# Two filler rates, an earlier feed-forward norm, a group norm over whole tiles and another order of the second half's products in an RWKV-7/mLSTM trunk

## The chip, the cores and the metric

The kernel runs on one core of a Trainium2 chip. Its engines work from queues of their own, each in program order: TensorE (PE, with its weight loads shown as PEld), VectorE (DVE), ScalarE (ACT), GpSimd (POOL) and SyncE (SP), which issues nearly all DMAs. The metric is the device time of one execution, in microseconds; lower is better. TensorE's clock is granted at one of two levels, 1.2 or 2.4 GHz; the profile shows the granted clock of a stretch as a share of the full one.

## What is computed

A two-layer trunk over 1024 tokens of width 1024. Layer 0 mixes tokens with RWKV-7, layer 1 with mLSTM, and each is followed by a SwiGLU feed-forward. The change touches layer 0's mixer and the start of its feed-forward:

```
xs = x[None] + xx[None] * mix[:, None, None, :]          # six mixes of each token with the one before
r, wl, k, v, al, gl = (xs[i] @ w_in[:, off:off + n] ...)  # receptance, decay, keys, values, rate, gates
decay = exp(-exp(-softplus(-(w0 + tanh(wl) @ w2)) - 0.5)); a = sigmoid(a0 + al @ a2); g = sigmoid(gl) @ g2
state = state * w_t + sa * b_t + v_t * k_t;  y = state @ r_t      # one step for each token
mu = mean(y, -1); var = mean(square(y - mu), -1)                  # over the 64 channels of a head
y = ((y - mu) * rsqrt(var + GN_EPS)) * gn_w + gn_b                # group norm
x = x + g1 * (((y + bonus) * g) @ w_out)
h = _rms(x) * (1.0 + sc2) + sh2;  x = x + g2 * swiglu(h)
```

## The kernel before

All data is float32, channels on the 128 partitions and tokens in two halves of 512 on the free axis. A large product is done in three matmuls, high part by high part, high by low and low by high: `split` makes the high part on ACT and the low part on DVE, for weights (128x1024) and operands (128x512) alike.

**The steps.** `chunks` runs the recurrence in 19 steps i = 0 to 18. Each of 16 blocks (8 head pairs of the first half of the tokens, then the 8 of the second) goes through `rw_prep` in step i, `rw_inverse` in step i+1, `rw_solve` in step i+2, and `rw_chain` and `rw_finish` in step i+3. `rw_chain` is serial: eight times it multiplies the state (PE, `c<-st,AR`), adds (DVE, tile `VU`), multiplies again (PE, `c<-VU,SR` and `c<-VU,KT`), and updates the state (DVE, tile `st`), while ACT copies the result to `Ys`. `rw_finish` takes the group norm of `Ys`, transposes it on PE, multiplies in the gates and stores it (`yd`). "Step 13" below means the stretch between the first `c<-st,AR` of the chain of i = 13 and that of i = 14.

**The filler.** Between these parts `run` draws dense products from `fillers`: the first half's values and gates, the second half's six products, the output projection of the first half, its feed-forward norm, and the first five column blocks of the feed-forward (`first`). Each `yield` reports units of PE work, some 24 matmuls of 512 columns for five of them, and `run(limit)` draws until `QUOTA` x (step + position) units are reached. `until` draws further wherever a step needs a product that isn't there. All fillers together are 317 units. `mixed` makes the operands of one product: for each of eight tiles one ACT scaling, one DVE multiply-add and a split, into the 18 buffers of the pool `a`, which hold one product's operands at a time. The products write PSUM tile `dn`.

**The order.** The instructions of an engine run in the order that the scheduler built, by data dependencies and by the place in the program. `ahead(part)` moves what it encloses forward by the number in `AHEAD`. When the steps are over, the pools are closed and opened anew (`FROOM`), and the output projection of the second half begins (`second`, `project`, with operands in `ga`).

Of the kernel before, what the change touches and what calls it, by code (L numbers as in the profile page):

```python
# [11 lines left out]
AF = mybir.ActivationFunctionType  # L12
ALU = mybir.AluOpType
ADD, SUB, MUL, MAX, MIN, POW = ALU.add, ALU.subtract, ALU.mult, ALU.max, ALU.min, ALU.pow
# [3 lines left out]
P = 128  # L18
# [9 lines left out]
DECAY = float(np.exp(-0.5))  # L28
CAP = 15.0
GROUPS = [(0, 5), (5, 5), (10, 4), (14, 4), (18, 4)]  # L30
QUOTA = 16
XW = 1
PT = "pt",
PA = "tmp",
# [4 lines left out]
POS = .25, .5, .75  # L39
# [1 line left out]
FEW = 3  # L41
LI = 3, 7, 7, 10
GT = "tmp", "tmp", "a", "ld"
AHEAD = dict(chain=50, mask=400, w=50, finish=50, pair=100, g=150, norm=500)


RES = {"x": (8, 520)}
# [82 lines left out]
class K:  # L130
# [98 lines left out]
    def ahead(self, part):  # L229
        n = AHEAD.get(part, 0)  # L230
        return self.tc.high_priority(n) if n else nullcontext()
# [425 lines left out]

    def rw_inverse(self, S):

        nc = self.nc
        SA, d0 = S["SA"], S["d0"]
        d1 = self.d1[self.nd1 % len(self.d1)]
# [68 lines left out]

    def rw_solve(self, S):

        nc = self.nc
        AR, SA = S["AR"], S["SA"]
        v = self.rload("v", S["j"], S["hf"])
        VU = self.t("VU", [P, 8, P])
# [34 lines left out]
        for e in range(2):  # L774
            nc.vector.tensor_copy(AR[:, e::2, self.rows(e)[1]], ps[e])
        S["VU"] = VU

# [22 lines left out]
    def rw_finish(self, S):  # L800

        nc = self.nc
        j, hf, Ys = S["j"], S["hf"], S["Ys"]
        y3 = Ys.rearrange("p u (h d) -> p (u h) d", h=2)
        m, v, jk = (self.t(n, [P, 64 if n == "gj" else 8]) for n in ("gm", "gv", "gj"))
        nc.vector.tensor_reduce(m, y3, mybir.AxisListType.X, ADD)
        nc.vector.tensor_scalar(m, m, -1.0 / 64, None, MUL)
        for q in range(8):
            nc.scalar.activation(jk, y3[:, q, :], AF.Square, bias=m[:, q:q + 1], accum_out=v[:, q:q + 1])
        nc.vector.tensor_scalar(v, v, 1.0 / 64, GN_EPS, MUL, ADD)  # L810
        nc.gpsimd.tensor_tensor(v, v, self.mhalf, POW)
        nc.vector.tensor_tensor(m, m, v, MUL)
        for q in range(8):
            nc.scalar.activation(y3[:, q, :], y3[:, q, :], AF.Identity, bias=m[:, q:q + 1], scale=v[:, q:q + 1])
        ps = self.bank("tr")
        for u in range(4):
            nc.tensor.transpose(ps[:, u * P:u * P + P], Ys[:, u, :], self.k_("ident"))
        bv = self.t("pt")
        nc.sync.dma_start(bv, self.bvd[j, hf])
        v = self.rload("v", j, hf)  # L820
        nc.vector.tensor_tensor(bv, bv, v, MUL)
        g = self.rload("g", j, hf)
        nc.vector.scalar_tensor_tensor(bv, ps, self.col("gn_w", j), bv, MUL, ADD)
        nc.vector.scalar_tensor_tensor(bv, bv, self.col("gn_b", j), g, ADD, MUL)
        nc.sync.dma_start(self.yd[hf][j], bv)
# [595 lines left out]
    def fillers(self, x0):  # L1421

        yield from self.rkv(0, "v")
        yield from self.gate(0)
        self.second_half()
        yield from self.lora(1, "s")
        yield from self.lora(1, "a")
        yield from self.rkv(1, "k")
        yield from self.rkv(1, "r")
        yield from self.rkv(1, "v")  # L1430
        yield from self.gate(1)
        for kt in range(KT):
            t = self.t("x")
            self.nc.sync.dma_start(t, self.A["xT"][kt, :, 0:HT])
            x0.append(t)
        while self.finished < 8:
            yield 0
        yield from self.project(self.yd[0], "wro", 0, x0, self.a0, PA)
        self.store(0, x0)
        self.norm_blocks(x0, 0, self.rstd(x0))  # L1440
        hp = []
        for x in x0:
            hi, lo = self.a0()
            self.split(hi, lo, x)
            hp.append((hi, lo))
        for n in range(EARLY[0][0], EARLY[0][1]):
            self.first(0, n, hp, ("mt", "tmp"))
            yield 11

    def chunks(self, x0):  # L1450
        fill = self.fillers(x0)
        self.pe = 0

        def step():
            w = next(fill, None)
            if w is None:
                return False
            self.pe += w
            return True

        def until(arr, j, hf):
            while self.done.get((arr, hf), 0) <= j:
                assert step()

        def run(limit):
            while self.pe < limit:
                n = self.pe
                if not step():
                    break
                if self.finished < 8 and self.pe == n and self.done.get(("g", 1)) == 8:  # L1470
                    break

        S = [None] * 16
        for i in range(19):
            if i >= 3:
                with self.ahead("chain"):
                    self.rw_chain(S[i - 3])
            run(QUOTA * (i + POS[0]))
            if 2 <= i < 18:
                until("v", (i - 2) % 8, (i - 2) // 8)  # L1480
                self.rw_solve(S[i - 2])
            run(QUOTA * (i + POS[1]))
            if 1 <= i < 17:
                self.rw_inverse(S[i - 1])
            run(QUOTA * (i + POS[2]))
            if i < 16:
                until("r", i % 8, i // 8)
                S[i] = self.rw_prep(i % 8, i // 8)
            run(QUOTA * (i + 1))
            if i >= 3:  # L1490
                until("g", (i - 3) % 8, (i - 3) // 8)
                with self.ahead("finish"):
                    self.rw_finish(S[i - 3])
                self.finished = i - 2
        while step():
            pass
# [188 lines left out]
```

## Time and profile before

| | us |
|---|---|
| median of 3 runs (lowest, highest) | 2932.73 (2917.15, 2933.27) |
| the profiled execution | 2919.56 |
| its span, first to last instruction | 2917.8 |
| PE busy | 2702.9 |
| DVE busy | 2036.1 |
| ACT busy | 1401.1 |

The span is what the engines took from the first to the last instruction; 1.8 us of the execution lie around it. An engine is busy while an instruction of its own executes. PE's busy time is no measure of speed alone: at the lower clock the same matmul takes twice as long and is busy all the while. The chains of steps 3 to 18 begin at 267.88, 318.58, 369.88, 433.77, 479.39, 516.42, 569.02, 610.01, 653.78, 715.49, 754.09, 793.62, 846.36, 882.95, 928.49 and 976.67 us.

### The profile page before, as it was taken

To read this page: it belongs to the slowest core of one execution; us is meant where nothing else is said; L and a number is where in the kernel's file an instruction comes from. 1 tells how busy PE (TensorE), PEld (TensorE's weight loads), DVE (VectorE), ACT (ScalarE), POOL (GpSimd) and SP (SyncE) were. 2 spreads that over 40 slices of the span, in tenths; PEclk is the share of its full clock that TensorE was granted. 3 is DMA by queue.
4 is the path that set the end of the run, shared out by engine and by line. 5 is a ranking of instruction groups with operands and counts; after the bars stand their busy time and mean duration, and the time that the engine had idled before them with its cause. 6 is when DMAs were issued, how large, how long until landed. Compare 5 with 4: busy or idle time off the path is not lost.

```text
span 2917.8 us, 46574 instructions
## 1 busy us (share of the span) xinstructions
PE 2702.9 (93%) x17080; PEld 2124.4 (73%) x17080; DVE 2036.1 (70%) x4029; ACT 1401.1 (48%) x2641; POOL 74.5 (3%) x98
## 2 busy tenths in 40 slices
PE   6899889999898999999999989999989999999988
PEld 5576556677676677887777767778867788887776
DVE  7877776877676468788877677665556865667645
ACT  5766786777666554322244354233435433323433
POOL 0000000000000000000000000000000000000000
PEclk9899789999798999999999989889989999999999
DMA  8775444455543455577788744345264322347734
GB/s 293 262 266 149 121 128 125 119 158 145 155 138 102 134 199 163 187 228 233 243 276 258 229 138 129 121 152 159 94 205 146 106 100 94 107 138 246 237 118 150
DMA packets 359721, 492.38 MB, mean 169 GB/s; under 512 B 125212, under 2 KB 208796, under 8 KB 359492
## 3 DMA queue, kind: packets, MB, share of 16 engines
q1 hardware_dynamic: 345668, 464.24, 50.1%
q10 hardware_dynamic: 13824, 25.17, 2.4%
q8 instruction: 134, 2.20, 0.3%
q14 instruction: 95, 0.78, 0.1%
HBM read 359.77 MB, written 129.50 MB: 168 GB/s over the span
## 4 chain that ended last, share of the span: by engine, by line
PE 61%; DVE 14%; DMA 11%; ACT 6%; issue 6%; POOL 1%; SPq 1%; DVEq 0%; POOLq 0%; ACTq 0%
PE dn L207 23%; PE c L207 20%; PE iv L207 7%; PE px L207 7%; PE sc L207 2%; DMA wraw<-wsd 2%; DMA tt<-gd 1%; DMA wraw<-in_wdn 1%; DVE wq L212 1%; DMA bgs<-in_ada 1%; DVE ga L212 1%; ACT wq L211 1%; DVE wlo L212 1%; PE tr L207 1%; ACT whi L211 1%
## 5 line engine op out<-in xcount | busy, mean ns | idle before, releaser
L207 PE MATMUL dn<-a,whi 128*128 128x512 f32 (+1 forms) x1200 | 434.4, 428 | 20.4 <-ACT a L211 8.0
L211 ACT ACTIVATE wq<-wraw 128x1024 fp32r<-128x1024 f32 x202 | 210.7, 1057 | 335.4 <-DVE wraw L889 89.6
L207 PE MATMUL c<-ga,wq 128*128 128x512 f32 x1446 | 354.2, 394 | 8.6 <-ACT ga L211 7.8
L207 PEld LDWEIGHTS c<-ga,wq 128*128 128x128 f32 x1446 | 271.5, 189 | 73.7 <-ACT ga L211 10.1
L212 DVE TENSOR_TENSOR wq<-wraw,wq 128x1024 fp32r<-128x1024 f32 x202 | 244.3, 1221 | 85.3 <-ACT wq L211 85.1
L207 PEld LDWEIGHTS dn<-a,whi 128*128 128x128 f32 (+1 forms) x1200 | 226.3, 196 | 81.8 <-ACT a L211 10.7
L207 PE MATMUL dn<-a,wlo 128*128 128x512 f32 (+1 forms) x664 | 275.1, 425 | 5.8 <-ACT wlo L443 2.9
L207 PE MATMUL c<-gb,wq 128*128 128x512 f32 x894 | 220.9, 399 | 9.4 <-DVE wq L212 6.4
L207 PEld LDWEIGHTS c<-gb,wq 128*128 128x128 f32 x894 | 169.2, 191 | 49.5 <-DVE wq L212 7.6
L207 PEld LDWEIGHTS dn<-a,wlo 128*128 128x128 f32 (+1 forms) x664 | 128.8, 197 | 37.1 <-issue 4.8
L211 ACT ACTIVATE whi<-wraw 128x1024 fp32r<-128x1024 f32 (+2 forms) x96 | 100.4, 1046 | 113.2 <-PE dn L207 81.9
L212 DVE TENSOR_TENSOR wlo<-wraw,whi 128x1024 fp32r<-128x1024 f32 (+2 forms) x96 | 116.0, 1208 | 45.7 <-ACT whi L211 39.7
L207 PE MATMUL iv<-ga,wq 128*128 128x512 f32 x552 | 136.0, 389 | 0.0
L207 PE MATMUL px<-ga,wq 128*128 128x512 f32 x528 | 128.7, 389 | 0.0
L211 ACT ACTIVATE w<-wraw 128x384 fp32r<-128x384 f32 (+1 forms) x100 | 56.7, 567 | 139.9 <-PE c L207 62.3
L207 PEld LDWEIGHTS iv<-ga,wq 128*128 128x128 f32 x552 | 103.6, 188 | 21.6
L207 PEld LDWEIGHTS px<-ga,wq 128*128 128x128 f32 x528 | 99.1, 188 | 20.7
L207 PE MATMUL dn<-gb,wq 128*128 128x512 f32 x426 | 104.1, 396 | 5.0 <-ACT gb L211 4.7
L207 PE MATMUL iv<-gb,wq 128*128 128x512 f32 x432 | 104.7, 390 | 0.0
L207 PEld LDWEIGHTS dn<-gb,wq 128*128 128x128 f32 x426 | 81.1, 191 | 23.9 <-ACT gb L211 5.3
L207 PE MATMUL c<-ga,w 128*128 128x512 f32 x372 | 93.4, 393 | 1.1 <-DVE ga L212 0.7
L1124 ACT ACTIVATE x<-x 128x512 f32<-128x512 f32 x77 | 48.3, 629 | 95.0 <-DVE x L933 44.9
(607 smaller groups left out, 5643.5 us busy)
## 6 DMA issues: line engine op xcount, KB each, us to landing
wraw<-in_wgu SPq DMA_DIRECT2D x110, 512.0 KB, 3.5
tt<-gd SPq DMA_DIRECT2D x154, 256.0 KB, 4.1
KT<-in_ada SPq DMA_DIRECT2D x40, 512.0 KB, 5.3
gd<-x SPq DMA_DIRECT2D x77, 256.0 KB, 2.0
gd<-tt SPq DMA_DIRECT2D x72, 256.0 KB, 2.1
wraw<-wsd SPq DMA_DIRECT2D x32, 512.0 KB, 4.7
bgs<-in_ada SPq DMA_DIRECT2D x96, 128.0 KB, 3.3
wraw<-in_wdn SPq DMA_DIRECT2D x24, 512.0 KB, 4.4
```

The source lines that it names most:

```text
L207: return self.nc.tensor.matmul(out, lhsT, rhs, start=start, stop=stop, **kw)
L211: self.nc.scalar.activation(hi, src, AF.Copy)
L212: self.nc.vector.tensor_tensor(lo, src, hi.bitcast(F32), SUB)
L1124: nc.scalar.activation(t, t, AF.Silu)
```

## The change

Four edits. The filler gets 19.6 units a step in the first 11 steps and 12.6 afterwards, in place of 16 throughout. The second half's products come as decay, keys, rate, receptance, gates, values, in place of decay, rate, keys, receptance, values, gates. The feed-forward norm of the first half and its split are moved forward in the schedule by 400. The group norm works on the whole 128x512 tile: DVE adds the negated mean, ACT squares once into a tile of the pool `pt`, DVE sums it and scales the tile, in place of eight ACT instructions that square and sum, and eight that scale and shift.

```
-QUOTA = 16
+
+QUOTA = 19.6, 12.6
-AHEAD = dict(chain=50, mask=400, w=50, finish=50, pair=100, g=150, norm=500)
+AHEAD = dict(chain=50, mask=400, w=50, finish=50, pair=100, g=150, norm=500, front=400)
@@ rw_finish
-        m, v, jk = (self.t(n, [P, 64 if n == "gj" else 8]) for n in ("gm", "gv", "gj"))
+        m, v = (self.t(n, [P, 8]) for n in ("gm", "gv"))
         nc.vector.tensor_reduce(m, y3, mybir.AxisListType.X, ADD)
         nc.vector.tensor_scalar(m, m, -1.0 / 64, None, MUL)
-        for q in range(8):
-            nc.scalar.activation(jk, y3[:, q, :], AF.Square, bias=m[:, q:q + 1], accum_out=v[:, q:q + 1])
+        nc.vector.tensor_tensor(y3, y3, m[:, :, None].to_broadcast([P, 8, 64]), ADD)
+        sq = self.t("pt", [P, 8, 64])
+        nc.scalar.activation(sq, y3, AF.Square)
+        nc.vector.tensor_reduce(v, sq, mybir.AxisListType.X, ADD)
         nc.vector.tensor_scalar(v, v, 1.0 / 64, GN_EPS, MUL, ADD)
         nc.gpsimd.tensor_tensor(v, v, self.mhalf, POW)
-        nc.vector.tensor_tensor(m, m, v, MUL)
-        for q in range(8):
-            nc.scalar.activation(y3[:, q, :], y3[:, q, :], AF.Identity, bias=m[:, q:q + 1], scale=v[:, q:q + 1])
+        nc.vector.tensor_tensor(y3, y3, v[:, :, None].to_broadcast([P, 8, 64]), MUL)
@@ fillers
         yield from self.lora(1, "s")
+        yield from self.rkv(1, "k")
         yield from self.lora(1, "a")
-        yield from self.rkv(1, "k")
         yield from self.rkv(1, "r")
+        yield from self.gate(1)
         yield from self.rkv(1, "v")
-        yield from self.gate(1)
...
-        self.norm_blocks(x0, 0, self.rstd(x0))
-        hp = []
-        for x in x0:
-            hi, lo = self.a0()
-            self.split(hi, lo, x)
-            hp.append((hi, lo))
+        with self.ahead("front"):
+            self.norm_blocks(x0, 0, self.rstd(x0))
+            hp = []
+            for x in x0:
+                hi, lo = self.a0()
+                self.split(hi, lo, x)
+                hp.append((hi, lo))
@@ chunks
+        def quota(x):
+            return QUOTA[0] * min(x, 11) + QUOTA[1] * max(x - 11, 0)
+
-            run(QUOTA * (i + POS[0]))
+            run(quota(i + POS[0]))
...
-            run(QUOTA * (i + 1))
+            run(quota(i + 1))
```

On PE, in the chain of step 13, the order before has the inverse of a later block (`iv`) and the products of `rw_prep` (`sc`, `c`<-`AR,KB`) between two rounds of the chain, and no filler:

```order
L207 MATMUL iv_8548<-XN_8535,SA_7990 16x16 x32
L207 MATMUL c_302_1589<-st_1582,AR_7432 128x128
L207 MATMUL iv_8585<-XB_8536,Y_1453_8547 16x16 x32
L207 MATMUL c_302_1589<-VU_8417,SR_7444 64x64 x2
L207 MATMUL c_302_1589<-VU_8417,KT_7489 64x64 x2
L207 MATMUL iv_8628<-XN_8535,SA_7990 32x32 x16
```

and the order of the changed kernel has output-projection products (`dn`) there:

```order
L208 MATMUL c_302_1589<-VU_8476,SR_7697 64x64 x2
L208 MATMUL c_302_1589<-VU_8476,KT_7742 64x64 x2
L208 MATMUL dn_8976<-a_8195,whi_8972 128x512
L208 MATMUL dn_8976<-a_8196,whi_8972 128x512
L208 MATMUL dn_8976<-a_8195,wlo_8973 128x512
L208 MATMUL dn_8976<-a_8201,whi_8972 128x512
L208 MATMUL dn_8976<-a_8202,whi_8972 128x512
L208 MATMUL c_302_1589<-st_1582,AR_7685 128x128
```

Fillers have moved into this place.

On PE, in the last chain (step 18), the order before has feed-forward products between the rounds:

```order
L207 MATMUL dn_11427<-a_10704,whi_11423 128x512
L207 MATMUL c_302_1589<-st_1582,AR_10325 128x128
L207 MATMUL dn_11427<-a_10703,wlo_11424 128x512
L207 MATMUL dn_11427<-a_10707,whi_11423 128x512
L207 MATMUL dn_11427<-a_10708,whi_11423 128x512
L207 MATMUL dn_11427<-a_10707,wlo_11424 128x512
L207 MATMUL c_302_1589<-VU_11166,SR_10337 64x64 x2
L207 MATMUL c_302_1589<-VU_11166,KT_10382 64x64 x2
```

and the changed kernel has the last inverse (`iv`), the last solve (`px`, `tr`) and then the chain with nothing between:

```order
L208 MATMUL iv_10949<-XD_10839,Y_1833_10929 32x32 x16
L208 MATMUL px_11096<-Z_11077,SA_10490 64x64
L208 MATMUL tr_11115<-SA_10490,AT_11069 64x64 x3
L208 MATMUL px_11096<-Z_11077,SA_10490 64x64 x15
L208 MATMUL tr_11115<-SA_10490,AT_11069 64x64 x5
L208 MATMUL c_302_1589<-st_1582,AR_10479 128x128
L818 MATMUL tr_11223<-kc,Ys_10994 128x128 x4
L208 MATMUL px_11116<-SA_10490,AT_11069 64x64 x8
L208 MATMUL c_302_1589<-VU_11061,SR_10491 64x64 x2
L208 MATMUL c_302_1589<-VU_11061,KT_10536 64x64 x2
L208 MATMUL c_302_1589<-st_1582,AR_10479 128x128
L208 MATMUL c_302_1589<-VU_11061,SR_10491 64x64 x2
```

All fillers now stand ahead of this chain; counted in the whole order, 130 of their matmuls stood behind its first row before, and none does now.

On DVE, in a group norm, the order before has the multiply that waits for POOL's power (L812) right behind the instruction that POOL waits for (L810), ahead of a chain's add (`VU`) and the masks (`SA`, `SR`):

```order
L810 TENSOR_SCALAR gv_8757<-gv_8757 128x8
L812 TENSOR_TENSOR gm_8756<-gm_8756,gv_8757 128x8
L787 TENSOR_TENSOR VU_8417<-c_302_1589,VU_8417 64x128
L631 TENSOR_TENSOR SA_8697<-sc_8699,kc 128x2x2x64
L631 TENSOR_TENSOR SR_8698<-sc_8699,kc 128x2x2x64
```

and the changed kernel has a sum (L812) and a scaling of the whole tile (L815) around the same wait:

```order
L812 TENSOR_REDUCE gv_7790<-pt_7794 128x8
L642 TENSOR_SCALAR br_7733<-kc,cc 128x128
L813 TENSOR_SCALAR gv_7790<-gv_7790 128x8
L788 TENSOR_TENSOR VU_7348<-c_302_1589,VU_7348 64x128
L815 TENSOR_TENSOR Ys_7247<-Ys_7247,gv_7790 128x512
L822 TENSOR_TENSOR pt_7805<-pt_7805,ld_7807 128x512
```

One instruction stands between L813 and L815 here.

## Rows read from the trace of the kernel before

**Rows 1.** The page: busy time, share of the span and instructions by engine.

```profile
PE 2702.9 (93%) x17080; PEld 2124.4 (73%) x17080; DVE 2036.1 (70%) x4029; ACT 1401.1 (48%) x2641; POOL 74.5 (3%) x98
```

**Rows 2.** Windows: stretch, length, busy per engine, granted clock, DMA share and rate.

```profile
191.58:267.88 76.30, 73.71 (x608) 56.60 (x607) 57.75 (x123) 48.45 (x81) 0.22 (x2) 1.00 0.63 183
267.88:433.77 165.89, 139.06 (x1482) 95.05 (x1481) 125.69 (x325) 129.37 (x277) 3.99 (x5) 0.85 0.44 127
433.77:569.02 135.25, 128.22 (x1498) 90.30 (x1497) 102.28 (x272) 93.66 (x227) 7.03 (x6) 0.95 0.43 123
569.02:715.49 146.47, 142.04 (x1616) 106.33 (x1613) 114.32 (x291) 102.21 (x255) 8.27 (x8) 1.00 0.53 149
715.49:846.36 130.87, 116.16 (x1399) 85.23 (x1397) 89.16 (x238) 87.67 (x221) 3.80 (x4) 0.84 0.50 150
846.36:976.67 130.31, 117.28 (x1429) 88.28 (x1426) 87.66 (x225) 80.51 (x204) 7.15 (x5) 0.90 0.41 117
976.67:1026.89 50.22, 40.31 (x236) 29.99 (x235) 23.75 (x46) 27.31 (x72) 3.27 (x2) 0.96 0.43 145
```

**Rows 3.** Windows, steps 13 and 16, all instructions.

```profile
754.09:793.62 39.53, 33.92 (x440) 25.53 (x441) 24.13 (x57) 25.66 (x71) 1.75 (x2) 0.70 0.50 161
882.95:928.49 45.54, 35.65 (x453) 27.64 (x450) 30.61 (x81) 27.33 (x70) 3.40 (x2) 0.78 0.41 118
```

**Rows 4.** Windows, fillers alone (tile dn; PE, PEld, DVE, ACT), steps 3 to 17.

```profile
267.88:976.67 708.79, 338.56 (x1083) 195.02 (x1082) 8.71 (x12) 44.11 (x73) 0.91 0.46 133
```

**Rows 5.** The chain that ended last: start, length, what; a run at full clock.

```profile
1051.39 10.88 PE c L207 x48
```

**Rows 6.** Waits, 290 to 420 us: who waited for whom, us, times, longest.

```profile
PEld dn L207 <- DVE a L212: 8.7, 13, 1.7
```

**Rows 7.** Timeline, 895 to 900 us: start, length, instruction, idle before and releaser.

```profile
895.14 0.17 DVE L812 TENSOR_TENSOR gm<-gm,gv 128x8 f32<-128x8 f32 x1 [1.44 <-POOL gv L811]
895.34 2.76 ACT L814 ACTIVATE Ys<-Ys,gm,gv 128x64 f32<-128x64 f32 x8 [1.18 <-DVE gm L812]
899.40 0.71 PE L207 MATMUL c<-st,AR 128*128 128x128 f32 x2 [4.47 <-ACT Ys L797]
```

**Rows 8.** Groups by line, 190 to 1030 us: busy us, mean ns, idle before.

```profile
L814 ACT ACTIVATE Ys<-Ys,gm,gv 128x64 f32<-128x64 f32 x128 | 45.5, 428 | 18.4 <-DVE gm L812 18.2
L809 ACT ACTIVATE gj<-Ys,gm 128x64 f32<-128x64 f32 x128 | 43.9, 343 | 11.2 <-DVE gm L807 9.0
L809 ACT ACTIVATION_READ_ACCUMULATOR gj<-Ys,gm 128x1 f32 x128 | 24.1, 188 | 0.0
L211 ACT ACTIVATE a<-mt 128x512 fp32r<-128x512 f32 x60 | 37.3, 622 | 3.0 <-DVE mt L412 2.1 <-ACT Ys L797 0.6
L806 DVE TENSOR_REDUCE gm<-Ys 128x8 f32<-128x512 f32 x16 | 10.8, 676 | 1.2 <-ACT Ys L797 1.2
L609 DVE TENSOR_TENSOR pt<-pt,pt 128x512 f32<-128x512 f32 x16 | 10.9, 683 | 0.3 <-ACT pt L608 0.3
```

**Rows 9.** Groups by line, whole span, POOL.

```profile
L811 POOL TENSOR_TENSOR gv<-gv,mhalf 128x8 f32<-128x8 f32 x16 | 30.7, 1917 | 506.5 <-DVE gv L810 436.0 <-DVE VU L787 37.9 <-DVE X L678 32.6
```

**Rows 10.** Timeline of PE, last chain to the first product behind it.

```profile
995.85 0.38 PE L207 MATMUL c<-st,AR 128*128 128x128 f32 x2
...
998.39 0.38 PE L207 MATMUL c<-st,AR 128*128 128x128 f32 x2
...
999.68 0.28 PE L207 MATMUL c<-VU,KT 128*64 128x64 f32 x2
...
1011.21 0.33 PE L817 MATMUL tr<-kc,Ys 128*128 128x128 f32 x1 [1.50 <-ACT Ys L814]
...
1025.82 0.79 PE L207 MATMUL c<-ga,wq 128*128 128x512 f32 x1 [7.05 <-ACT ga L211]
```

**Rows 11.** DMA issues, 995 to 1042 us: KB each, median us to landing.

```profile
tt<-yd SPq DMA_DIRECT2D x8, 256.0 KB, 4.4
gd<-tmp SPq DMA_DIRECT2D x2, 256.0 KB, 2.0
```

More of the change, by code (lines that the diff above doesn't have):

```diff
@@ L1481, in chunks @@
                 self.rw_solve(S[i - 2])
-            run(QUOTA * (i + POS[1]))
+            run(quota(i + POS[1]))
             if 1 <= i < 17:
                 self.rw_inverse(S[i - 1])
-            run(QUOTA * (i + POS[2]))
+            run(quota(i + POS[2]))
             if i < 16:
```

## The prediction

> **What bounds the kernel now.** The page comes first. PE is busy 93% of the span, DVE 70%, ACT 48% [rows 1], so PE is the engine to follow, and a change pays where PE idles or runs slow. The change touches the recurrence alone, so I next read windows cut at the first multiply of each third chain [rows 2]. From 267.88 to 976.67 us (steps 3 to 17, 708.8 us) the reader is to see two losses in each row: the length less PE's busy time, and the length times what the granted clock lacks to 1. Steps 3 to 5 lose 165.9 - 139.1 = 26.8 us of idle and 165.9 x 0.15 = 24.9 us of clock, 51.7 together. Likewise steps 6 to 8 lose 7.0 + 6.8 = 13.8, steps 9 to 11 4.4 + 0, steps 12 to 14 14.7 + 20.9 = 35.6, and steps 15 to 17 13.0 + 13.0 = 26.0. The sum is 131.5 us: 66 idle, 65.5 clock. The other 577 us are PE's work at full clock. The fillers are 1083 matmuls of 512 columns [rows 4]; 48 of them take 10.88 us at full clock [rows 5], 0.227 each, so 246 us. The remaining 331 us are the recurrence's own work, 22.1 a step.
>
> Where the losses lie tells their cause. Steps 13 and 16 alone lose 17.5 (5.6 + 11.9) and 19.9 us (9.9 + 10.0) [rows 3]: in the order before they hold 17 and 26 fillers, against 72 a step on average. Step 13 is starved because `until` drew gates and values early in step 11, step 16 because the norm stands between the projection and the first feed-forward product. In steps 3 to 5 fillers exist but wait for operands: four `mixed` (gates, decay, rate, keys) fall between units 40 and 76, steps 2.5 to 4.75 at 16 a step, and PE's filler weight loads wait 8.7 us in 13 pieces for DVE's split [rows 6]. Steps 9 to 11 hold two `mixed` as well, but with 300 fillers, and lose only 4.4. So losses come with thin or late filler, and the clock is at its lower level, 1.2 GHz, for part of just those stretches.
>
> **The change, part by part.** *Filler.* Counted in the built order of PE, steps 3-5, 6-8, 9-11, 12-14 and 15-17 hold 197, 215, 300, 171 and 199 fillers before, and 261, 280, 233, 231 and 192 after. That is 115 more inside, 15 more ahead of step 3, and none of the 130 behind the first row of the last chain. Work moved in: 115 x 0.227 = 26.1 us, and 15 x 0.227 = 3.4 us ahead, where PE is busy 73.7 of 76.3 us at full clock [rows 2]. Their weights' loads come earlier on SP's queue too; the DMA engines are busy 41 to 53% in steps 3 to 17 [rows 2], so I cost that at nothing. Late loads would show as ACT waiting for `wraw`.
>
> *What the losses become.* The trace has no row for this, so I bound them: at least 22 us (every group like steps 9 to 11), at most 131.5 (nothing gained). Within that I take each group by its nearest row. Steps 3 to 5 now hold two `mixed` (decay, keys) instead of most of four, and ACT is freed (below): half of 51.7, 26. Steps 6 to 8 hold two (rate, receptance) instead of one: 13.8 grows to 22. Steps 9 to 11 (gates, values) have 67 fillers fewer: 9, between their own 4.4 and 13.8. Steps 12 to 14 lose the starved step: of 35.6 the 17.5 of step 13 goes, and of the other 18.1, mostly the wait for the projection's operands, a third goes too: 12. Steps 15 to 17 have the norm early, so step 16's 19.9 goes and 6 stays, but the last inverse and solve now stand bare ahead of the last chain, which I estimate at half of step 16's loss, whose like stretch stood bare too, 10 us: 16. The sum is 85, against 131.5: -46.5 us.
>
> *Group norm.* Removed from ACT, each time: eight squares of 343 ns with accumulator reads of 188, and eight scalings of 428 [rows 8], 7.7 us, for one whole-tile square, priced as the copy of the same size, 0.62: 7.1 x 16 = 113 us less on ACT. DVE gets an add, a sum and a scaling of 512 columns, 0.68 each [rows 8], for one small multiply of 0.17 [rows 7]: 1.9 x 16 = 30 us more. ACT is never the sole bound of the five groups [rows 2], so its 113 us go off the path in the main; they pay where the chain waits behind them. Rows 7 shows that: DVE waits 1.44 us for POOL, then eight scalings hold ACT 2.76 us, the copy of `Ys` comes late and PE idles 4.47 us. Such waits are inside the 46.5. The wait of DVE for POOL stays, about 1.9 us a norm [rows 9] less what stands between; in the new order that is at most 2.1 us of work and mostly one short instruction, so DVE loses perhaps 0 to 10 us more in all. I take 0 on the path, since DVE has 26% of room in steps 3 to 17 (519 of 709 us busy, [rows 2]); its share becomes (519 + 30 + 9 for the added fillers' splits) / 688 = 81%. Queued behind it are the chain's add, the masks and the splits. Every group norm also takes one more `pt` buffer of four, whose earlier user is a factor of the same `rw_prep`, long read: nothing.
>
> *The end.* Before, from the last chain's first row to the first projection product is 976.67 to 1025.82, 49.1 us [rows 2, 10], and 130 fillers run in it (29.5 us). After, it is bare. A round takes 2.54 us with few fillers in it [rows 10]; eight of them, some at the lower clock, 21.6. From the chain's end (999.96) to the first transpose, 11.25 us before [rows 10], the new norm needs copy 0.3, sums 2 x 0.68, add and scaling 2 x 0.68, square 0.62, small ones 0.4, POOL 1.9 and some 0.9 of signals: 6.8. Transposes take 0.7. Then two DVE operations (1.5), the store of `yd` (2.0, as the like `gd`), the load (4.4) [rows 11], split and signals (2.6) make 10.5, during which PE can do the 21 products of the other seven operands, 4.8. The sum is 34.8: -14.3 us. Bounds: 30, and 44 if the projection's operands arrive no sooner than before.
>
> *Norm ahead* costs no instruction; its gain is step 16's. A new order can change how often ACT loads tables; that is hidden on an engine that is idle 30% of steps 3 to 17.
>
> The sum: +3.4 + 26.1 - 46.5 - 14.3 = -31.3 us on the profiled 2919.6 (span 2917.8 and 1.8 around it): 2888. The median shown is 13.2 above that execution. Of the four known executions two lie near 2918 and two at 2933, so I add half, 6.6: **2895 us**. Medians of this kernel tell about 1% from no change, 29 us: below 2903 counts as faster.
>
> **A rule against the rows.** Idle and lower clock go together in rows 2 and 3. The Trainium skill, "TensorE: Matmul & The Clock Gate" (Terms), puts the penalty of the lower clock at the throttled time times the missing share: that would make the 65.5 us above wholly recoverable. The trace agrees only in part: in rows 7 PE waits 4.47 us at the time the clock is low in step 16, and a wait costs the same at either clock.
>
> **Rivals.** (1) *The clock stays full.* All 65.5 us of clock loss go and a third of the idle 66: losses of 44, the end as above, so 2888 - 41 = 2847, with the offset 2854. For it: steps 9 to 11 ran at 1.00 throughout. Against: 24 fillers in step 6 and 41 in step 9 of the new order. By the page's rule just named, the clock's part of it follows. Chance 0.12. (2) *The losses only move.* Rate and receptance wait for operands in steps 6 to 8 as decay and keys did, losses stay near 120: 2888 + 35 = 2923, with the offset 2930. For it: `a` still holds one product's operands. Against: starved steps 13 and 16 are filled whatever else happens. Chance 0.27. (3) *Slower: DVE becomes the bound.* DVE waits for POOL with the chain's add behind it, and its 30 us more, with 5 more of waiting, land on the path while losses stay at 131.5: 3.4 + 26.1 - 14.3 + 35 = +50, 2970, with the offset 2976. It decides once losses pass 145 us (+28.7), DVE then being nearly always what PE waits for. Against: steps 9 to 11 ran with DVE busy 78% at a loss of 3%. Chance 0.12, for 2960 and more as for 2976. The sum above has 0.49, with losses of 65 to 105 us, so 2875 to 2915.
>
> **The numbers.** The range goes from 2857 to 2932: it holds the sum's cases (0.49), rival 2 nearly whole (0.25) and the upper half of rival 1 (0.06). Faster by over 1%: three quarters of the sum's cases and rival 1, 0.49. Within 1%: the rest of the sum's cases and rival 2, 0.39. Slower: 0.12.
>
> **What would show it.** Windows from the first chain to the last should show losses of some 85 us, steps 13 and 16 at a clock above 0.9, and steps 3 to 5 shorter than 155 us though they hold 64 more fillers. ACT should be busy some 113 us less, DVE 30 more. The last chain should run without `dn` in about 22 us, the first `ga` product following within 15. It is wrong if a group loses what it lost before, if PE's longest waits are for the new scaling (L815), or if the end takes as long as before.

## The result, and the profile after

The changed kernel takes 2961.04 us (median of 4 runs, 2956.66 to 2965.10), the kernel before 2929.65 beside it: a ratio of 1.0119 with a 95% interval of 1.0098 to 1.0141. The change makes it slower by 1.2%, 31 us, where the prediction had 2895 us.

The page of the changed kernel answers to [rows 1]:

```profile
PE 2715.5 (92%) x17080; PEld 2133.0 (72%) x17080; DVE 2064.4 (70%) x4061; ACT 1326.4 (45%) x2276; POOL 72.4 (2%) x98
```

The span is 2959.6 us, 41.8 more than before; some 10 of these are chance, because the profiled execution of before was 10 us under its median. DVE is busy 28 us more (30 were said), ACT 75 less (113 were said).

Windows cut at the same places as [rows 2]: the stretch ahead of step 3, steps 3 to 5, 6 to 8, 9 to 11, 12 to 14 and 15 to 17, and the last chain up to the first `ga` product.

```profile
191.58:273.50 81.92, 77.76 (x632) 59.68 (x630) 60.24 (x133) 50.94 (x83) 0.22 (x2) 0.98 0.61 178
273.50:443.09 169.59, 153.34 (x1543) 104.73 (x1541) 126.16 (x306) 112.35 (x214) 3.98 (x5) 0.88 0.42 125
443.09:604.03 160.94, 143.68 (x1552) 104.11 (x1551) 122.48 (x297) 102.91 (x199) 5.63 (x6) 0.90 0.46 132
604.03:743.14 139.11, 126.32 (x1503) 94.58 (x1503) 102.34 (x262) 80.82 (x167) 5.25 (x6) 0.94 0.55 161
743.14:897.63 154.49, 134.25 (x1518) 99.32 (x1517) 117.67 (x310) 77.84 (x160) 7.13 (x7) 0.88 0.41 115
897.63:1019.04 121.41, 112.10 (x1404) 82.96 (x1402) 83.93 (x212) 63.99 (x134) 7.57 (x5) 0.92 0.46 133
1019.04:1055.76 36.72, 16.49 (x104) 12.10 (x105) 19.81 (x40) 8.86 (x21) 1.95 (x1) 0.50 0.35 114
```

Counted as in the prediction (idle of PE plus what the clock lacks), the five groups lose 36.6, 33.4, 21.1, 38.8 and 19.0 us, 148.9 together, against 131.5 before and 85 predicted. Steps 3 to 17 take 745.5 us instead of 708.8. (The measure counts idle time at the lower clock one and a half times; so below I give PE's idle time and the clock apart.)

The whole of steps 3 to 17 in one window, first of the kernel before, then of the changed one, and the fillers alone (tile `dn`) of the changed one, which answer to [rows 4]:

```profile
267.88:976.67 708.79, 642.77 (x7413) 465.19 (x7413) 519.11 (x1350) 493.42 (x1180) 30.24 (x28) 0.91 0.46 133
```

```profile
273.50:1019.04 745.54, 669.68 (x7513) 485.70 (x7511) 552.58 (x1385) 437.92 (x869) 29.57 (x29) 0.90 0.46 132
...
273.50:1019.04 745.54, 364.85 (x1198) 217.62 (x1197) 12.75 (x18) 47.87 (x79) 0.90 0.46 132
```

The reader is to see where the 36.8 us come from. The fillers are busy 364.85 us instead of 338.56, 26.3 more, about what was put on the 115 that were moved in (26.1). PE's idle time did not shrink by it; it grew from 66.0 to 75.9 us, and the clock fell from 0.91 to 0.90.

Steps 9, 13, 14 and 16 of the changed kernel; 13 and 16 answer to [rows 3]:

```profile
604.03:649.27 45.24, 35.97 (x448) 26.29 (x448) 33.73 (x94) 26.13 (x56) 1.75 (x2) 0.82 0.47 136
793.19:838.18 44.99, 42.12 (x501) 30.76 (x499) 36.16 (x93) 23.16 (x48) 2.12 (x2) 0.96 0.49 142
838.18:897.63 59.45, 46.67 (x511) 35.19 (x508) 44.20 (x120) 31.59 (x64) 3.26 (x3) 0.77 0.33 92
938.15:983.28 45.13, 43.37 (x513) 31.21 (x509) 35.06 (x100) 24.09 (x50) 3.28 (x2) 1.00 0.46 131
```

Steps 13 and 16 are cured, as said (clocks of 0.96 and 1.00 for 0.70 and 0.78). But steps 9 and 14 now run at 0.82 and 0.77, with 9.3 and 12.8 us idle. In step 14 the fillers stop for 29 us, from the last product of the projection to the first one of the feed-forward, with the feed-forward norm between (eight multiplies on DVE, eight scalings on ACT):

```profile
843.95 0.39 PE L208 MATMUL dn<-a,wlo 128*128 128x512 f32 x1
...
864.86 4.87 DVE L862 TENSOR_TENSOR x<-x,sc 128x512 f32<-128x512 f32 x8 [1.71 <-PE sc L208]
866.80 5.73 ACT L863 ACTIVATE x<-x,mod,scp 128x512 f32<-128x512 f32 x8
...
873.11 0.79 PE L208 MATMUL dn<-a,whi 128*128 128x512 f32 x1 [1.61 <-ACT a L212]
```

In the kernel before, the same place lay in step 16 and took 36 us:

```profile
894.53 0.40 PE L207 MATMUL dn<-a,wlo 128*128 128x512 f32 x1
...
930.80 0.79 PE L207 MATMUL dn<-a,whi 128*128 128x512 f32 x1 [0.57 <-ACT a L211]
```

So this gap did not close: it shrank from 36 to 29 us and moved, with the fillers around it, from step 16 to step 14.

The end: windows of the 20 us from the first `ga` product on, of before and of the changed kernel.

```profile
1025.82:1045.82 20.00, 19.72 (x73) 15.69 (x74) 17.51 (x23) 13.08 (x19) 0.00 (x0) 0.83 0.86 305
```

```profile
1055.76:1075.76 20.00, 15.68 (x50) 11.82 (x51) 7.31 (x11) 5.79 (x10) 0.00 (x0) 0.81 0.56 197
```

From the last chain to the first `ga` product it takes 36.7 us instead of 49.1, 12.4 less (14.3 were said). But then PE does 50 matmuls in 20 us instead of 73; at 19.72 / 73 = 0.27 each that gives 6 us back. The timeline of PE in the last chain and behind it answers to [rows 10]:

```profile
1026.71 0.80 PE L208 MATMUL c<-st,AR 128*128 128x128 f32 x2 [0.79 <-ACT Ys L798]
1029.55 0.79 PE L208 MATMUL c<-st,AR 128*128 128x128 f32 x2 [0.76 <-ACT Ys L798]
...
1052.33 1.08 PE L818 MATMUL tr<-kc,Ys 128*128 128x128 f32 x4 [9.39 <-DVE Ys L815]
1055.76 0.79 PE L208 MATMUL c<-ga,wq 128*128 128x512 f32 x1 [2.34 <-ACT ga L212]
```

A round takes 2.84 us, at a clock of 0.50 throughout (the last of the windows above); then PE waits 9.4 us for the new scaling.

### The profile page after: what moved, and what is told of

It reads as the page before. It is cut to its first block, busy times and chain, and to the rows that moved or that the text cites. A ratio compares the mean times of both kernels' runs of the same rounds, so it can differ in the third digit from the quotient of the medians.

```text
span 2959.6 us, 46255 instructions
## 1 busy us (share of the span) xinstructions
PE 2715.5 (92%) x17080; PEld 2133.0 (72%) x17080; DVE 2064.4 (70%) x4061; ACT 1326.4 (45%) x2276; POOL 72.4 (2%) x98
## 4 chain that ended last, share of the span: by engine, by line
PE 56%; DVE 17%; DMA 12%; issue 8%; ACT 5%; SPq 1%; POOL 1%; DVEq 0%; ACTq 0%; POOLq 0%
PE dn L208 21%; PE c L208 18%; PE iv L208 7%; PE px L208 6%; DMA tt<-gd 2%; PE sc L208 2%; DVE wq L213 1%; DMA wraw<-in_wdn 1%; DMA bgs<-in_ada 1%; DMA bgs<-in_wdn 1%; DMA wraw<-wsd 1%; DMA wsd<-bgs 1%; DVE wlo L213 1%; DMA st<-in_ada 1%; DVE ga L213 1%
## 5 line engine op out<-in xcount | busy, mean ns | idle before, releaser
L213 DVE TENSOR_TENSOR wlo<-wraw,whi 128x1024 fp32r<-128x1024 f32 (+2 forms) x96 | 116.0, 1209 | 38.8 <-ACT whi L212 34.4
L208 PEld LDWEIGHTS px<-ga,wq 128*128 128x128 f32 x528 | 99.0, 188 | 20.8
L208 PEld LDWEIGHTS iv<-gb,wq 128*128 128x128 f32 x432 | 81.8, 190 | 17.5 <-DVE x L934 0.3
```

Of the source, the lines that this page charges most:

```text
L208: return self.nc.tensor.matmul(out, lhsT, rhs, start=start, stop=stop, **kw)
L213: self.nc.vector.tensor_tensor(lo, src, hi.bitcast(F32), SUB)
```

## The experiments

Eighteen kernels, each timed in three rounds beside the kernel before. `a_` stands for the changed kernel with something altered, `b_` for the kernel before. Length, PE's idle time and clock are those of steps 3 to 17 in the profiled execution.

| kernel | median us | ratio to before [95%] | length | idle | clock |
|---|---|---|---|---|---|
| before | 2926.91 to 2929.75 | 1 | 708.8 | 66.0 | 0.91 |
| after | 2961.04 | 1.0119 [1.0098, 1.0141] | 745.5 | 75.9 | 0.90 |
| `a_oldgn` | 2958.99 | 1.0111 [1.0085, 1.0137] | 741.3 | 69.8 | 0.90 |
| `a_oldquota` | 2956.96 | 1.0096 [1.0072, 1.0119] | 744.3 | 88.2 | 0.88 |
| `a_oldorder` | 2942.13 | 1.0052 [1.0034, 1.0070] | 726.6 | 62.7 | 0.92 |
| `a_nofront` | 2967.82 | 1.0137 [1.0118, 1.0157] | 754.6 | 68.6 | 0.88 |
| `b_order` | 2943.31 | 1.0048 [1.0027, 1.0070] | 722.1 | 81.5 | 0.90 |
| `b_quota` | 2944.38 | 1.0054 [1.0034, 1.0075] | 728.2 | 65.2 | 0.92 |
| `b_gn` | 2928.90 | 1.0003 [0.9987, 1.0019] | 718.4 | 68.8 | 0.89 |
| `b_front` | 2914.33 | 0.9963 [0.9943, 0.9984] | 692.9 | 64.1 | 0.93 |
| `a_keysold` | 2958.54 | 1.0099 [1.0072, 1.0126] | 735.3 | 75.1 | 0.92 |
| `a_valsold` | 2938.45 | 1.0037 [1.0021, 1.0054] | 729.4 | 64.8 | 0.91 |
| `a_knlate` | 2961.64 | 1.0116 [1.0099, 1.0133] | 742.8 | 66.1 | 0.89 |
| `a_mid400` | 2969.40 | 1.0142 [1.0123, 1.0161] | 743.8 | 77.4 | 0.91 |
| `a_gmid` | 2962.75 | 1.0105 [1.0066, 1.0145] | 742.0 | 75.3 | 0.91 |
| `b_gates` | 2940.61 | 1.0044 [1.0021, 1.0067] | 730.2 | 72.0 | 0.88 |
| `b_frontgn` | 2927.68 | 0.9999 [0.9981, 1.0018] | 714.1 | 66.5 | 0.90 |
| `b_front17` | 2938.68 | 1.0039 [1.0019, 1.0059] | 715.7 | 58.8 | 0.91 |
| `b_frontdve` | 2952.64 | 1.0077 [1.0052, 1.0102] | 735.4 | 75.6 | 0.87 |
| `b_front15` | 2947.60 | 1.0058 [1.0039, 1.0077] | 729.6 | 68.6 | 0.87 |

One profiled execution may lie far from its kernel's median: `b_front`'s was 14 us under, `b_quota`'s 10 and `b_gates`' 19 above. How far chance reaches within a trace, `b_gates` shows: up to 528 us PE runs the same instructions in the same order there as in the kernel before. Its steps 3 to 5, to be set against the row 267.88:433.77 of [rows 2]:

```profile
268.02:440.64 172.62, 146.70 (x1483) 99.43 (x1482) 125.94 (x325) 129.43 (x277) 3.99 (x5) 0.79 0.44 125
```

The same work with the same idle time (25.9 us for 26.8) took 6.7 us longer at a clock of 0.79 for 0.85, a loss of 62.2 us for 51.7. So times are compared by medians, and traces for where, not for how much; a difference of 10 us in the loss of one group may be chance.

**Each part undone.** Each kernel takes one of the four edits out of the changed kernel, as the hunks of the diff show.

```
a_oldgn      rw_finish as before
a_oldquota  -QUOTA = 19.6, 12.6     +QUOTA = 16, 16
a_oldorder   fillers: decay, rate, keys, receptance, values, gates
a_nofront   -... norm=500, front=400)   +... norm=500)
```

> The changed kernel with the group norm of before (sixteen small ACT instructions, one small DVE multiply), all else as changed. Theory D (DVE is what PE waits for, since the norm moved 30 us of work there): about 30 us faster than the changed kernel, near 2930, and PE's waits for DVE in steps 3 to 17 fall from 46 us towards the 30 of before. Theory Q (the two rates move 115 fillers into steps that cannot take them): no faster than the changed kernel, 2955 to 2975, since ACT gets its 113 us back.

> The changed kernel with 16 units a step throughout, all else as changed; in its built order 134 fillers stand behind the first row of the last chain again, 1078 in steps 3 to 17. Theory Q: back to 2930 or below, since steps 3 to 17 lose 119 fillers (27 us) and the last chain is covered again. Theory D: at most 10 us faster than the changed kernel, as the same DVE work remains.

> The changed kernel with the second half's products in the order of before (decay, rate, keys, receptance, values, gates). Theories D and Q: within 10 us of the changed kernel's 2961. A third theory, O (the new order itself puts rate and receptance together in steps 6 to 8, whose losses went from 14 to 33 us): 20 us faster, near 2940, with steps 6 to 8 losing less than 20 us.

> The changed kernel without moving the feed-forward norm ahead. All theories: slower than the changed kernel by 5 to 20 us, about 2970, as its built order has 23 fillers in step 14 in place of 67 and the starved stretch of step 16 of before returns there. If it is the norm's early place that holds up DVE (steps 12 to 14 lose 39 us in the changed kernel): faster, 2945 to 2955.

The old group norm and the old rate give 2 and 4 us, inside the intervals: neither alone is the cause. The norm ahead is worth 7. The old order gives 19 us:

```profile
275.73:1002.35 726.62, 663.89 (x7513) 482.29 (x7511) 550.78 (x1385) 438.96 (x870) 30.21 (x29) 0.92 0.47 136
```

Idle falls from 75.9 to 62.7, and steps 6 to 8 lose 2.9 us instead of 33.4, while steps 3 to 5 lose 47.2 instead of 36.6. The order is the largest of the four, but some 13 us over before remain.

**Each part alone**, in the kernel before.

```
b_order   fillers: decay, keys, rate, receptance, gates, values
b_quota  -QUOTA = 16   +QUOTA = 19.6, 12.6   (with quota(x))
b_gn      rw_finish as in the changed kernel
b_front   norm_blocks and its split inside self.ahead("front"), front=400
```

> The kernel before with the new product order alone; one rate of 16, old norm, old group norm. If the order is what costs (undoing it in the changed kernel gave 19 us back, with a loss of 2.9 us in steps 6-8 instead of 33.4), this is slower than before: 2945 to 2955, the loss of steps 3-17 well above the 131.6 of before and steps 6-8 over 30. If the order costs only beside the two rates, it is within 8 us of before and steps 6-8 stay near 14.

> The kernel before with the two rates alone; old order, old group norm, norm not ahead. What the prediction said of the rates by themselves: +3.4 +26.1 for fillers moved, losses down by up to 46, the end 14 shorter. If the rates do that, under 2915. If the losses only move and the end has lost its cover, 2930 to 2945, with the loss of steps 3-17 at 100 to 130 and the stretch from the last chain to the feed-forward products at 50 or more, nearly all of it loss.

> The kernel before with the new group norm alone. Putting the old one back in the changed kernel moved the time by 2 us, so here: within 10 us of before, with DVE's busy time in steps 3-17 about 30 us higher and ACT's about 60 lower. A theory in which DVE's longer share of the finish is what delays the other work gives 2945 or more.

> The kernel before with the feed-forward norm ahead alone. In the changed kernel the step ahead was worth 7 us. Here: 2919 to 2925, the gain between the last chain and the first feed-forward product (49.1 in the kernel before). If its cover there is the fillers behind the last chain and nothing waits for the norm, no change.

Order +14 us, rates +16, group norm 0, norm ahead -11 to -13. **The rates** are the part that the prediction counted on. Steps 3 to 17 and the end of `b_quota`, as windows:

```profile
274.42:1002.61 728.19, 663.00 (x7528) 483.11 (x7527) 527.82 (x1353) 510.76 (x1200) 28.09 (x28) 0.92 0.48 137
1002.61:1043.46 40.85, 16.79 (x90) 11.07 (x88) 18.53 (x39) 18.63 (x58) 4.27 (x2) 0.50 0.26 86
1043.46:1063.46 20.00, 16.68 (x47) 11.63 (x48) 7.04 (x10) 5.55 (x9) 0.00 (x0) 0.73 0.57 194
```

Idle is 65.2 us, against 66.0 before: the fillers moved in fill no idle time, and the stretch grows by 19.4 of their 26.1 us, at a clock of 0.92 for 0.91. The end saves 8.3 us, and the next 20 us lose 26 matmuls of 73, 7 us. So of the 29.5 us that the 130 fillers behind the last chain's first row take (0.227 each), the end gives about 1 back: there they had been nearly free. Steps 3 to 5 hold 277 fillers instead of 197 and lose no less (59.8 us for 51.7): filler was not what they lacked.

**The norm ahead** gains, in its profiled execution, by the clock:

```profile
266.17:959.05 692.88, 628.81 (x7407) 453.71 (x7407) 519.10 (x1350) 493.66 (x1173) 30.37 (x28) 0.93 0.48 136
```

Idle stays (64.1 for 66.0), while PE is busy 14 us less for the same work, at a clock of 0.93 for 0.91; how much of this is chance (the execution lay 14 us under the median) is open. The gap between projection and feed-forward shrinks from 36 to 21 us; step 16 loses 16.2 us for 19.9 and step 17 0.7 for 6.2, and the end, where the gain was expected, is no shorter (51.8 us for 49.1). At 2914.33 us this is the fastest kernel of the study, faster than the kernel before and the changed one by its interval.

**Which half of the order.** Two swaps make the new order, and two pauses of the big products stand in that part of the changed kernel's trace: none begins between 468 and 490 us (step 6) or between 607 and 624 (step 9). (The longest pause, that of step 14, has no experiment of its own; in `a_gmid` below it falls into two of 16 and 10 us, and step 14 still loses 30.2.) Timeline rows around the first:

```profile
467.33 0.48 PE L208 MATMUL dn<-a,whi 128*128 128x512 f32 x1
...
489.70 1.22 PE L208 MATMUL dn<-a,wlo 128*128 128x512 f32 x2
```

```profile
482.58 0.26 ACT L542 ACTIVATE tmp<-tmp 128x64 f32<-128x64 f32 x1
...
484.11 0.60 ACT L439 ACTIVATE tmp<-dn 128x512 f32<-128x512 f32 x1
```

The rate product's first stage is over within a microsecond of the first row, but ACT copies it (L439) only at 484.11, behind the keys' norm (L542), whose values come back from DRAM. In step 9 the split between the two stages of gates lies likewise behind other work of DVE. Four kernels put these to the test.

```
a_keysold   fillers: decay, rate, keys, receptance, gates, values
a_valsold   fillers: decay, keys, rate, receptance, values, gates
a_knlate   -                self.kk_norm(ss, hf)
           +                if hf == 0: self.kk_norm(ss, hf)
           +                else: self.late = ss
            yield from self.lora(1, "a")
           +self.kk_norm(self.late, 1)
a_mid400   +mid=400; the middle steps of lora and gate inside self.ahead("mid")
```

> The changed kernel with keys put back behind rate (decay, rate, keys, receptance, gates, values); the other half of the new order stays. In the changed kernel's trace the big products stop for 21 us in step 6, where the rate product's middle step lies behind the norm of the keys. If that pause costs: losses of steps 6 and 7 go from 14 and 17 to under 5 together, steps 9 and 10 keep theirs (17 and 2), and the time is 2940 to 2950. If the order costs through gates ahead of values: 2955 to 2965.

> The changed kernel with values put back ahead of gates (decay, keys, rate, receptance, values, gates); keys stay ahead of rate. In the changed kernel's trace the big products stop for 17 us in step 9, between the two stages of the gates product. If that pause costs: the loss of step 9 goes from 17 to under 5, steps 6 and 7 keep theirs, and the time is 2945 to 2955. If only the place of the keys costs: 2955 to 2965.

> The changed kernel with its new order, but the second half's norm of the keys written out behind the rate product instead of ahead of it, so that ScalarE copies the rate's middle result before it waits for the norm's values to come back from DRAM. If the pause of step 6 comes from that wait: it shrinks from 21 us to under 10, the losses of steps 6 and 7 fall from 31 to 10 to 20, and the time is 2940 to 2955. If the pause comes from the mixing of the product's inputs, or the order costs otherwise: no change, 2956 to 2966.

> The changed kernel with the middle steps of the two-stage products (rate, decay, gates: ScalarE's copy, the splits of it and of the second weights) written out 400 instructions ahead, as the norm is. If the pause of step 9 is the middle step that lies behind a burst of VectorE's other work: it shrinks from 17 us to under 6, the loss of step 9 falls from 17 to under 6, and the time is 2945 to 2956. If the pauses only move with the work that is put off for it: 2956 to 2966.

Values ahead of gates gives 22 us, keys behind rate 2.5. With keys behind rate, steps 6 to 8 do lose 3.3 us instead of 33.4, but steps 3 to 5 lose 9 more and steps 12 to 14 8 more. The five groups together lose 133.0 us for 148.9 in this execution, while the median gains only 2.5. So the loss moves at least in part; how much, a single trace doesn't tell. `a_knlate` puts a price on the pause. Steps 6 and 7 of the changed kernel, then of `a_knlate`:

```profile
443.09:484.14 41.05, 32.38 (x451) 23.34 (x450) 33.47 (x80) 27.09 (x57) 2.12 (x2) 0.86 0.40 106
484.14:562.21 78.07, 70.59 (x776) 50.63 (x776) 51.90 (x137) 48.92 (x97) 1.75 (x2) 0.88 0.46 134
```

```profile
444.32:489.88 45.56, 38.33 (x450) 27.21 (x449) 35.15 (x94) 27.70 (x56) 2.12 (x2) 0.81 0.42 118
489.88:558.88 69.00, 64.59 (x585) 46.76 (x583) 51.53 (x121) 43.61 (x81) 2.12 (x2) 0.85 0.43 126
```

The pause shrank from 21 us to about 5, and PE idled 11.6 us in the two steps instead of 16.2; their clock was lower, 0.81 and 0.85, they took 4.6 us less, step 8 took 6.6 more, and the whole time did not change. So the theory that this pause sets the time falls. `a_mid400` was slower by 8, as long as its longer stretch ahead of step 3 (89.6 for 81.9 us), where the first half's products were moved too.

**Gates again, and the sums.**

```
a_gmid       as a_mid400, for the second half's gate alone
b_gates      fillers: decay, rate, keys, receptance, gates, values
b_frontgn    b_front with the new rw_finish
b_front17    b_front with QUOTA = 17
```

> The changed kernel with the middle step of the second half's gates product alone written out 400 instructions ahead; the rest of the new order stays. The big products issued in steps 9 and 10 become 80 and 96 instead of 41 and 135. If the gates' pause is what their place costs (values ahead of gates gave 22 us): the loss of step 9 falls from 17 to under 6, steps 9 and 10 take 90 to 95 us instead of 102, and the time is 2940 to 2952. If a pause that is closed only comes up elsewhere, as with the keys: 2956 to 2966, with the loss of the other steps up by what step 9 loses.

> The kernel before with gates ahead of values in the second half, nothing else. If the swap costs by itself: 2937 to 2950, the whole of what both swaps cost in the kernel before (14 us). If it costs only beside the higher first rate: within 5 us of before, and the place of the keys is what costs at the rate of 16.

> The kernel before with the feed-forward norm ahead and the new group norm; old order, one rate of 16. If parts add: 2915 (the norm ahead gave 13 us, the group norm nothing). If VectorE's longer share of the finish eats what the norm ahead gives: 2922 or more.

> The kernel before with the feed-forward norm ahead and one rate of 17: 48 big products stay behind the last chain instead of 136. If fillers moved ahead cost about 0.17 us each whatever the rate, as the two rates alone showed, and the end is 4 to 8 shorter: 2918 to 2930. If unevenness was what the two rates cost: 2900 to 2912, with the loss of steps 3-17 under 100.

`b_gates` costs 14 us, as much as both swaps: gates ahead of values is what the order costs there. At a rate of 16 a cause shows in the fillers alone (tile `dn`) of steps 10, 15 and 16, first before, then `b_gates`:

```profile
610.01:653.78 43.77, 26.63 (x93) 16.14 (x93) 0.00 (x0) 2.34 (x4) 1.00 0.56 162
846.36:882.95 36.59, 18.13 (x63) 10.92 (x63) 1.49 (x2) 0.00 (x0) 1.00 0.51 135
882.95:928.49 45.54, 7.57 (x26) 4.66 (x26) 1.48 (x2) 0.00 (x0) 0.78 0.41 118
```

```profile
614.04:695.17 81.13, 50.74 (x172) 31.75 (x172) 0.00 (x0) 8.07 (x14) 0.89 0.53 156
863.74:911.25 47.51, 14.80 (x45) 8.27 (x44) 2.24 (x3) 0.00 (x0) 0.80 0.40 111
911.25:951.48 40.23, 2.24 (x4) 1.12 (x4) 0.00 (x0) 0.00 (x0) 0.71 0.38 103
```

Step 10's solve needs the first values, so `until` draws the whole of gates ahead of it: 172 fillers in one step, which takes 81 us instead of 44, and fewer are left for steps 15 and 16. Step 10 loses 16.7 us for 1.2 and step 15 20.8 for 0.3; step 16 had lost 19.9 before and loses 19.5. `a_oldquota`, which has this order and rate too, holds 175 fillers in its step 10, and that may be why the old rate gives so little back in the changed kernel. (This reading was not tested apart.) In the changed kernel, whose rate is higher, `until` draws nothing there, and yet values first gives 22 us. `a_gmid` closes the gates' pause in step 9, and the time stays; steps 9 to 11 take 4.2 us less, steps 12 to 14 3.8 more. What the swap costs at the higher rate stays open.

`b_frontgn` is also the changed kernel with the old order and the old rate, so the medians make a path: before 2927, norm ahead 2914, group norm 2928, two rates 2942 (`a_oldorder`), order 2961. That the group norm costs 13 beside the norm ahead and nothing alone shows that the parts don't add: the four alone sum to +0.7%, together they are +1.2%. A rate of 17 costs 24 us against `b_front`, so unevenness is not what the two rates cost.

**VectorE's time, and the other direction.**

```
b_frontdve   b_front, in rw_finish ahead of the sum over y3:
            +for _ in range(2):
            +    nc.vector.tensor_tensor(y3, y3, y3, MAX)
b_front15    b_front with QUOTA = 15
```

> The kernel with the norm ahead (2914) and in each of the 16 finishes two more VectorE operations of 128x512 (0.68 us each), which leave the values as they are: 22 us more of VectorE, as much as the new group norm adds in steps 3-17 (540 for 519), with ScalarE's work as before. If VectorE's time is what the group norm cost beside the norm ahead: 2923 to 2935. If it was the finish written another way, with other waits: 2910 to 2920.

> The kernel with the norm ahead (2914) and a rate of 15 for 16: 15 big products fewer in steps 3-17, 10 more behind the last chain, the rest ahead. If each moved ahead costs 0.17 to 0.30 us and one behind the last chain nothing: 2908 to 2914. If the early steps (3-5 have 167 for 197) then stand bare: 2915 to 2925.

Two DVE operations more in each finish, 22 us in all, make the kernel 38 us slower. The built order changed with them (the five groups hold 196, 216, 304, 159 and 201 fillers for 197, 215, 300, 171 and 193), and no run tells the price of the operations from that of the order. Steps 3 to 17 of `b_frontdve`, to be set against the row of `b_front` above:

```profile
267.72:1003.07 735.35, 659.77 (x7408) 477.87 (x7407) 534.18 (x1378) 498.16 (x1175) 28.25 (x28) 0.87 0.45 128
```

PE does the same 7408 matmuls. It idles 11.5 us more and is busy 31.0 us more, at a clock of 0.87 for 0.93: the larger part of the difference is the clock's. (The two executions lie 52 us apart, their medians 38; 9 of these 14 us lie behind the first `ga` product.) PE's waits in these steps, of `b_front` and then of `b_frontdve`, show two that grew:

```profile
PE c L207 <- DVE VU L787: 6.2, 8, 1.3
...
PE c L207 <- ACT Ys L797: 3.4, 8, 1.1
```

```profile
PE c L207 <- DVE VU L787: 9.4, 11, 1.5
PE c L207 <- ACT Ys L797: 7.7, 14, 2.2
```

The chain waits 7.5 us longer for its own add on DVE and for its copies on ACT. That both stand behind the finish in their queues is argued, not shown. The new group norm adds more to DVE's busy time (25.0 us for 18.1, from the pages of `b_frontgn` and `b_frontdve` against `b_front`), yet costs 13 us, not 38, beside the norm ahead. That the difference is what ACT's relief is worth, and that `b_gn`'s net of nothing is two large terms against each other, is a guess that no run tests.

A rate of 15 costs 33 us, though 15 fillers fewer stand in steps 3 to 17. Slower on both sides of 16: the number moved does not set the time. Where each filler falls may: at a rate of 15 steps 9 to 11 hold 349 of them for 300 and lose 28.4 us for 4.0.

Seven of the eighteen times lie outside every range that was expected of them: `b_front`, `a_valsold` and `b_order` are 5, 7 and 2 us faster, `a_mid400`, `b_front17`, `b_frontdve` and `b_front15` 3, 9, 18 and 23 us slower. The last three had been priced by what earlier runs had cost for each filler or group norm moved.

## Why the prediction was wrong

*What was moved.* Right: 115 fillers for 26.1 us measured 26.3, the stretch ahead of step 3 +5.6 for +3.4. That the first agrees so well is in part luck: a filler took 0.31 us on the average before and 0.30 after (364.85 / 1198), not 0.227.

*What the losses become.* This is the step that failed: 148.9 us for 85. The prediction read the losses as thin or late filler and healed each group by the fillers and the `mixed` that it would hold: 26, 22, 9, 12 and 16 us, where 36.6, 33.4, 21.1, 38.8 and 19.0 were measured. `b_quota` shows the fault: 115 fillers more, the same idle time. The two starved steps were filled as said (17.5 and 19.9 us became 5 and 2), but steps 6, 7, 9 and 14 lost 14, 17, 17 and 26, for 4, 1, 1 and 12 before. In step 14 stands the gap at the norm that the prediction had taken out with step 16. With the old order at the new rates the losses are 120.9 us: of the 46.5 some 11 came (131.5 - 120.9), and 28 went to the order. The order had only +8 for steps 6 to 8 and +5 for steps 9 to 11 in the sum; in steps 3 to 17 it costs 19 us, in the profiled executions (745.5 for 726.6) as in the medians. Why the new order loses so much at the new rates stays open.

*Group norm.* Nothing on the path was right for the edit alone; beside the norm ahead it costs 13. The reason given, that DVE has 26% of room, is in doubt since `b_frontdve`, where 22 us on DVE came with 38, new order included. ACT's 113 us were 75, in part because durations that overlap were added (the 128 scalings of 428 ns in [rows 8] are busy 45.5 us, not 54.8).

*The end.* 12.4 us of the 14.3 came, up to the first `ga` product. The term stopped there, though, and the next 20 us gave about half back. The last chain, bare, ran at 0.50, the lower level of 1.2 GHz, a round took 2.84 us for the 2.54 assumed, and PE waited 9.4 us from the chain to the transposes for 6.8. This wait is for the new scaling (L815) and the longest of PE between step 3 and the first `ga` product: one of the signs of being wrong that the prediction named. Another came too, since three groups lost more than before.

*Norm ahead.* Right in its sign, 7 us beside the other edits and 11 to 13 alone, but step 16's 19.9 did not go: alone, step 16 still loses 16.2, and in the changed kernel the gap is step 14's.

*The rule.* Idle and lower clock went together step by step, as the prediction had it (12.8 us idle at 0.77 in step 14, 1.8 at 1.00 in step 16), but not kernel by kernel: `a_keysold` idles 75.1 us at 0.92, `b_front15` 68.6 at 0.87. The Trainium skill, "TensorE: Matmul & The Clock Gate" (Terms), puts the clock's price at the throttled time times the missing share: 735.4 x 0.13 - 692.9 x 0.07 = 47 us between `b_front` and `b_frontdve`, an estimate by that rule. The trace agrees in kind, with 31.0 us more busy time for the same matmuls; the estimate also counts the time in which PE idles at the low clock, and the clocks in it are rounded to two digits (the clock records of the two traces hold 99.0 and 184.3 us at the lower level in these steps, which makes 42.6).

*The rivals.* The second, that losses only move, named what `a_keysold` and `a_knlate` hint at, but at 120 us of losses and 2930. The third had the sign and the bound (slower past 145 us of losses) and 2976; but DVE's added time is not what made the change slow, since undoing the group norm gave 2 us.

## What to carry over

Before filler is moved to where an engine idles, ask whether it can start there: if the idle time stands beside waits for operands, more filler is paid at most of its price (19.4 of 26.1 us in `b_quota`). Work that lies behind the last step of a serial chain may cost nothing where it is, and its removal is to be counted until the engine is back at full rate, not to the first instruction behind it. On a serial path, price a vector instruction by adding one, and look at what it shifts in the order: the idle share of its engine gave 0 here, the run 38 us for 22.

## What the runs showed of the hardware

Of the kernel before, 25 executions in one job lie between 2912.5 us, at a mean granted clock of 0.952, and 2941.9, at 0.941: 1% between executions of one program, which goes with the clock (the correlation over the 25 is -0.83).

So do the kernels. By the medians over each one's executions, the mean granted clock goes from 0.952 (`b_front`) over 0.947 (before) and 0.940 (the changed kernel) to 0.936 (`a_nofront`). Time multiplied by what the clock lacks to 1 goes from 140 to 190 us, the rest of the time only from 2771 to 2791. Of the 31 us that the change costs, 22 are such clock loss (2961.04 x 0.060 - 2929.65 x 0.053), idle time at the low clock included. So the kernels differ more in what they lose to the clock than in all the rest; what sets the clock of each, the runs don't show.

Closing a pause of 21 us in the fillers left the time as it was, with the clock of these steps lower in the profiled execution (`a_knlate`, 0.81 and 0.85 for 0.86 and 0.88). And 22 us more of DVE, with the order that came of it, made the whole 38 us longer at the same number of matmuls, mostly through a clock of 0.87 for 0.93.
